# A build-time list scheduler for a two-layer hybrid trunk: a shared-port rule for VectorE and GpSimd, and matmul prices from measurement

## The chip, the cores and the metric

The kernel runs on one core of a Trainium2 chip. The metric is the device time of one execution in microseconds (us), as a median over several runs. The engines are named as the profile names them: PE is TensorE's matmul stream and PEld its weight loads, DVE is VectorE, ACT is ScalarE, POOL is GpSimd, SP is SyncE, which issues all the DMAs here.

## The reference, cut to what matters

A float32 input of 1024 tokens by 1024 channels passes through two layers of the same form and a last RMSNorm. Cut to its outline:

```python
for l in range(2):
    h = rmsnorm(x, norm_mix[l])
    parts = split(h @ w_in[l])
    y_a = rglru_mixer(...)    # causal convolution, gated linear recurrence
    y_b = nsa_mixer(...)      # compressed, selected and sliding-window attention
    y_c = gla_mixer(...)      # gated linear attention in chunks
    y_d = mla_mixer(...)      # latent attention
    x = x + groupwise_rmsnorm(y_a, y_b, y_c, y_d) @ w_out[l]
    h = rmsnorm(x, norm_ffn[l])
    gate, up = split(h @ w_gate_up[l])
    x = x + (silu(gate) * up) @ w_down[l]
return rmsnorm(x, final_norm)
```

## The kernel before, in words

**Precision.** Most products are made of three passes over operands that are split in a high and a low part (fp32r): ACT casts the source to the high part, DVE subtracts that from the source and writes the low part (`split`, line 382). One such split of a 128x512 tile therefore costs one ACT and one DVE instruction. Some sources lie in PSUM (then the DVE subtraction has one SBUF operand), others in SBUF (then it has two).

**Stages of a layer.** (1) The input norm and the first projections; (2) gated linear attention (`z_stream`, `gla_levels`, `gla_out`, from line 776), whose products are in plain float32, with projections of other mixers as filler for PE; (3) compression of keys and values, and projections; (4) latent attention (`mla_a`, `mla_t`, `mla_pv`); (5) sparse attention (`nsa_a`, `nsa_t`, `nsa_pv`); (6) the rest of the output projection beside the second norm (`h_stream`, `forms`, from line 1905), which writes the seven Strassen-like forms of the normed input; (7) the gate and up projections, as seven half-size products per 256 columns (`mat`, line 2149), whose weight forms are made by `prepare` (line 2059): GpSimd adds or subtracts two weight blocks in SBUF (a 128x512 product, tiles `utmp`, `qtmp` and `stg`), then ACT and DVE split the result; (8) the down projection in the same manner (`chunks`, line 2286), where both operands must be split. The last columns follow (`down`), and after the second layer the final norm (`finish`, line 2394).

**What sets the order.** Nothing is reordered on the chip: each engine runs its own list of instructions in order. These lists are written at build time by the class `Flow` (line 175), a list scheduler with a clock per engine. DVE, ACT and POOL operations are put in with a priority, a price and their dependences (`do`, line 193; `D_` and `P_` in lines 297 to 301 set the prices, 0.07 us + n/960 on DVE for n columns). PE work comes from generators ("streams") that yield the time at which they can go on, and book the price of what they issued with `f.pe(price)` (line 199). `run` (line 226) takes again and again the candidate with the smallest key, and emits it:

```python
c = self.clk.get(eng, 0.0)
r = when(o[3], eng)
key = (max(c, r + load), o[0], r, o[1])
```

that is the earliest start by the planner's clock, then the priority (a small number first), then the time at which its inputs were ready, then the order of entry. `when` (line 78) adds a latency to what another engine made: 0.12 us on the same engine, 0.26 us towards PE, 0.19 us otherwise. So a price has no effect on the chip but through the order in which instructions of one engine stand, and through the choice of buffers and PSUM banks, which goes by the same clock. The arithmetic of all RMSNorms goes through `rstd_of` (line 441): DVE writes `ms`, GpSimd raises it to the power -0.5 (`rstd`), and a DVE operation scales the rows by it.

Of the kernel before, what the change touches and what calls it, by code (L numbers as in the profile page):

```python
# [76 lines left out]

def when(x, eng):
# [7 lines left out]
    return 0.0 if x is None or x is True else float(x)  # L86

# [87 lines left out]
class Flow:  # L175
# [7 lines left out]

    def __init__(self):
        self.clk = {}
        self.t = 0.0
        self.streams = []
        self.ops = {}
        self.n = 0
        self.tag, self.prio = None, 0  # L190
        self.table = ("Exp", "Tanh")

    def do(self, eng, cost, deps, func, a, k, table=None):
        self.n += 1
        ev = Ev(eng)
        self.ops.setdefault(eng, []).append((self.prio, self.n, cost, deps, func, a, k, ev, self.tag, table))
        return ev
# [28 lines left out]
    def run(self, until):  # L226

        while not until():
            best = None
            for eng, q in self.ops.items():  # L230
                c = self.clk.get(eng, 0.0)
                for o in q:
                    r = when(o[3], eng)
                    load = 1.28 if o[9] is not None and o[9] != self.table else 0.0
# [15 lines left out]
            else:  # L250
# [5 lines left out]
                self.clk[eng] = o[7].t = start + o[2]  # L256
                o[4](*o[5], **o[6])  # L257

@with_exitstack
def kernel(ctx: ExitStack, tc: tile.TileContext, I: dict, out: bass.AP, dbg=None):  # L260
# [180 lines left out]
    def rstd_of(ss, n, count, deps):  # L441
# [3 lines left out]
        return r, P_(172, e, G.tensor_tensor, r[:, :n], ms[:, :n], negh[:, :n], ALU.pow)  # L445
# [134 lines left out]
    def cm(g, m, evac, last=False):  # L580
# [3 lines left out]
        for k in range(NK):  # L584
# [8 lines left out]
            te = f.pe(6 * 0.216)  # L593
# [41 lines left out]
    def start_stage(l, ready, load, gain, hp, bufs, bd, vpl, tables=0.0, done=None):  # L635
# [36 lines left out]
        def g2(gq):  # L672

            for hf in range(2):
                cs = slice(hf * 512, (hf + 1) * 512)
                for m in range(2):
# [3 lines left out]
                    for k in range(NK):  # L680
# [6 lines left out]
                        te = f.pe(3 * 0.216)  # L687
# [53 lines left out]
    for l in range(DEPTH):  # L741
# [34 lines left out]
        def z_stream():  # L776
# [4 lines left out]
            for hf in range(2):  # L781
# [11 lines left out]
                tg = D_(512, f.pe(0.858), V.tensor_scalar, z[:, cs], pz, par["bg2"], -320.0, ALU.add, ALU.max)  # L793
# [5 lines left out]
            for hf in range(2):  # L799
# [32 lines left out]
        def a_stream(c, xc, tx):  # L832
            tg, tt = [], []
            for gi in range(2):
                tg.append(ap.tile([P, SEQ], F32, tag=f"tg{gi}", name=f"tg{gi}"))
                for hf in range(2):
# [4 lines left out]
                    e = A_(512, [f.pe(0.858), par["done"]], S.activation, tg[gi][:, cs], pg, AF.Tanh, bias=halfb[:, c, gi:gi + 1],  # L841
# [11 lines left out]
            e = D_(1024, e, V.tensor_tensor_scan, xc, a, ti, 0.0, ALU.mult, ALU.add)  # L853
# [85 lines left out]
        def gla_levels():  # L939
# [3 lines left out]
            for t in range(NT):  # L943
                for li in range(5):
# [34 lines left out]
        def gla_out():  # L979
# [3 lines left out]
            for t in range(NT):  # L983
# [6 lines left out]
                if t < NT - 1:  # L990
# [13 lines left out]
                    td = D_(256, f.pe(0.432), V.tensor_tensor, ds, dsv,  # L1004
# [11 lines left out]
                te = f.pe(1.29)  # L1016
# [126 lines left out]
        def compress():  # L1143
# [5 lines left out]
            for j in range(2):  # L1149
# [11 lines left out]
                for u in range(4):  # L1161
# [4 lines left out]
                    for q_ in range(4):  # L1166
# [8 lines left out]
                        te = f.pe(0.22)  # L1175
# [36 lines left out]
            te = f.pe(0.7)  # L1212
# [1273 lines left out]
```

## Time and profile before

| | us |
|---|---|
| median of 3 runs | 2569.16 |
| lowest and highest of them | 2566.72, 2569.29 |
| the profiled execution, its own time | 2567.09 |
| its span, first to last instruction | 2565.0 |
| PE busy in the span | 2486.2 |
| DVE busy | 1907.0 |
| ACT busy | 1234.1 |
| POOL busy | 716.3 |

The profiled execution lies 2.07 us under the median. Busy time on PE is the union of matmuls whose ends are modelled, so a PE that counts as busy may still be waiting for short times between two matmuls. The mean granted clock of PE over the span was 0.990.

### The profile page before, as it was taken

Reading aid. Unit: us, or ns where it says so; the run is one execution under the profiler, and the core shown is the slowest. Engines: PE = TensorE matmul, PEld = TensorE weight load, DVE = VectorE, ACT = ScalarE, POOL = GpSimd, SP = SyncE. Lnnn points to the kernel's source line nnn. Section 1 sums busy time; section 2 is a strip of 40 time slices with the busy share of each in tenths; the row PEclk is TensorE's granted clock in tenths of the full one; section 3 lists DMA queues with packets and bytes.
Section 4 is the critical chain, followed back from the end, with each engine's and each line's share of the span. In section 5 each row is a group of like instructions: output and inputs, shape, how many; then the busy total and the mean of one; then the engine's idle time right before and its main releaser. Section 6 shows DMA issues by size and latency. Waiting matters only on the chain.

```text
span 2565.0 us, 35737 instructions
## 1 busy us (share of the span) xinstructions
PE 2486.2 (97%) x12629; PEld 2077.9 (81%) x12629; DVE 1907.0 (74%) x3654; ACT 1234.1 (48%) x2727; POOL 716.3 (28%) x698
## 2 busy tenths in 40 slices
PE   8999899998999999999999998999989999999998
PEld 7777788887888888778887787888878888887786
DVE  7985987787665665798769768877776566667976
ACT  5444587874333333444344446877653333334443
POOL 2010111223333333543110101212143333336422
PEclk9999999999999999999999999999999999999999
DMA  4011102221232333543310111031302332335432
GB/s 156 17 46 43 53 26 81 65 85 36 87 107 95 107 104 97 211 162 99 123 65 17 62 35 46 26 95 54 116 22 82 115 115 79 111 121 196 156 91 91
DMA packets 137410, 224.05 MB, mean 87 GB/s; under 512 B 13552, under 2 KB 83600, under 8 KB 134672
## 3 DMA queue, kind: packets, MB, share of 16 engines
q1 hardware_dynamic: 137232, 221.77, 26.3%
q8 instruction: 100, 1.64, 0.3%
q14 instruction: 78, 0.64, 0.1%
HBM read 164.07 MB, written 49.28 MB: 83 GB/s over the span
## 4 chain that ended last, share of the span: by engine, by line
PE 83%; DVE 9%; ACT 3%; issue 2%; DMA 1%; SPq 1%; POOL 1%; DVEq 0%; POOLq 0%; ACTq 0%
PE ps L2167 32%; PE ps L2308 13%; PE ps L609 7%; PE ps L1796 4%; PE ps L1345 4%; PE ps L590 3%; PE ps L1739 2%; PE ps L1720 2%; DVE T L257 2%; PE ps L685 2%; PE ps L628 2%; PE ps L2333 1%; PE ps L1536 1%; PE ps L1512 1%; DVE x_res L257 1%
## 5 line engine op out<-in xcount | busy, mean ns | idle before, releaser
L2167 PE MATMUL ps<-T,wu 128*128 128x512 f32 (+1 forms) x2160 | 498.6, 386 | 3.1 <-ACT qtmp L257 1.8
L2167 PEld LDWEIGHTS ps<-T,wu 128*128 128x128 f32 x2160 | 401.2, 189 | 86.6 <-ACT qtmp L257 2.0
L2167 PE MATMUL ps<-h,wu 128*128 128x512 f32 (+1 forms) x1656 | 386.0, 386 | 0.5 <-DVE wu L257 0.5
L2167 PEld LDWEIGHTS ps<-h,wu 128*128 128x128 f32 x1656 | 302.2, 188 | 68.9 <-DVE wu L257 0.7
L257 POOL TENSOR_TENSOR rstd<-ms,negh 128x1 f32<-128x1 f32 (+1 forms) x152 | 100.0, 661 | 778.8 <-DVE ms L257 778.4
L2308 PE MATMUL ps<-T 128*128 128x512 f32 x1176 | 275.7, 390 | 3.9 <-DVE x_res L257 3.8
L2308 PEld LDWEIGHTS ps<-T 128*128 128x128 f32 x1176 | 220.8, 188 | 52.9 <-DVE x_res L257 4.2
L609 PE MATMUL ps<-w,T 128*128 128x512 f32 (+1 forms) x1152 | 250.9, 366 | 2.1 <-DVE KS L257 1.1
L257 ACT CAST wu<-stg 128x512 fp32r<-128x512 f32 x220 | 136.2, 619 | 189.3 <-PE ps L2167 80.3
L609 PEld LDWEIGHTS ps<-w,T 128*128 128x128 f32 x1152 | 191.5, 189 | 35.4 <-issue 4.3
L257 POOL TENSOR_TENSOR utmp<-stg,stg 128x512 f32<-128x512 f32 x84 | 114.5, 1364 | 344.6 <-DVE wu L257 130.5
L257 DVE TENSOR_TENSOR wu<-stg,wu 128x512 fp32r<-128x512 f32 x214 | 182.4, 852 | 14.2 <-ACT wu L257 14.2
L1796 PE MATMUL ps<-w,T 128*128 128x512 f32 x768 | 190.7, 396 | 0.0
L257 DVE TENSOR_TENSOR wu<-utmp,wu 128x512 fp32r<-128x512 f32 x134 | 110.2, 823 | 107.9 <-ACT wu L257 101.3
L257 DVE TENSOR_TENSOR x_res<-x_res,ps 128x512 f32<-128x512 f32 x224 | 143.2, 678 | 34.9 <-PE ps L2308 18.5
L1796 PEld LDWEIGHTS ps<-w,T 128*128 128x128 f32 x768 | 140.4, 188 | 26.9
L257 DVE TENSOR_TENSOR pts<-ps,pts 128x512 fp32r<-128x512 f32 x212 | 140.8, 685 | 26.9 <-ACT pts L257 25.5
L257 ACT CAST wu<-utmp 128x512 fp32r<-128x512 f32 x134 | 83.2, 621 | 118.2 <-POOL utmp L257 118.2
L257 POOL TENSOR_TENSOR stg<-stg 128x512 f32<-128x512 f32 x88 | 129.9, 1495 | 3.5
L257 ACT CAST pts<-ps 128x512 fp32r<-128x512 f32 x212 | 118.2, 591 | 16.3 <-PE ps L1720 12.9
L257 ACT CAST T<-stg 128x512 fp32r<-128x512 f32 x116 | 70.9, 621 | 105.8 <-PE ps L2308 91.3
L257 DVE TENSOR_TENSOR T<-stg,T 128x512 fp32r<-128x512 f32 x108 | 102.7, 957 | 25.3 <-ACT T L257 25.0
(378 smaller groups left out, 4799.5 us busy)
## 6 DMA issues: line engine op xcount, KB each, us to landing
stg<-in_w_gate_up_dram SPq DMA_DIRECT2D x88, 512.0 KB, 3.9
stg<-af SPq DMA_DIRECT2D x70, 512.0 KB, 3.6
af<-so SPq DMA_DIRECT2D x20, 1024.0 KB, 6.1
stg<-in_w_in_dram SPq DMA_DIRECT2D x36, 512.0 KB, 3.5
br<-in_w_down_dram SPq DMA_DIRECT2D x24, 512.0 KB, 6.5
af<-sg SPq DMA_DIRECT2D x20, 512.0 KB, 2.7
stg<-in_cmp_w_dram SPq DMA_DIRECT2D x16, 512.0 KB, 3.9
stg<-in_w_out_dram SPq DMA_DIRECT2D x16, 512.0 KB, 3.9
```

The lines of the kernel that those rows point to most:

```text
L257: o[4](*o[5], **o[6])
L590: PE.matmul(o[:, hf * 512:(hf + 1) * 512], lhsT=w[:, a], rhs=T[:, b, k, hf * 512:(hf + 1) * 512], start=(k == 0 and i == 0), stop=(k == NK ...
L609: PE.matmul(o[j][:, :g.n], lhsT=T[:, a, k, t * P:(t + 1) * P], rhs=g.of(k)[:, b, :], start=(k == 0 and i == 0), stop=(k == NK - 1 and i == 2))
L628: PE.matmul(o[:, :g.n], lhsT=T[:, a, k, t * P:(t + 1) * P], rhs=g.of(k)[:, b, :], start=(k == 0 and i == 0), stop=(k == NK - 1 and i == 2))
L685: PE.matmul(o, lhsT=w[:, a], rhs=T[:, b, k, cs], start=(k == 0 and i == 0), stop=(k == NK - 1 and i == 2))
L1345: PE.matmul(st[:, o0:o0 + wp_], lhsT=lh, rhs=rh[:, k0 + c0:k0 + c0 + wp_], start=(i == 0), stop=(i == len(ops) - 1), skip_group_check=True)
L1512: PE.transpose(pt[:, (2 * j + i) * P:(2 * j + i + 1) * P], Pm[:, i, kb * P:(kb + 1) * P], ident)
L1720: PE.transpose(pt[:, h * P:(h + 1) * P], Ps[h // 2][:, h % 2, kb * P:(kb + 1) * P], ident)
L1739: PE.matmul(ot, lhsT=VS[:, kb0 + kb, br].rearrange("p a d -> p (a d)"), rhs=R["npts", t, br, kb][:, a], start=(kb == 0 and a == 0), stop=( ...
L1796: PE.matmul(o, lhsT=T[:, a, 2 * u + k, t * P:(t + 1) * P], rhs=w.w[:, b_, k * 512:k * 512 + 512], start=(n == 0), stop=(n == 6 * len(us) - 1))
L2167: PE.matmul(bk[b, i][:, cs], lhsT=u[:, x, k * P:(k + 1) * P], rhs=H[n][:, y, k, cs], skip_group_check=True, start=(start and k == 0 and s ...
L2308: PE.matmul(o, lhsT=a[:, x, t * P:(t + 1) * P], rhs=b[:, y], skip_group_check=True, start=(new and s == 0), stop=(k == k0 + nk - 1 and s = ...
```

## The change

The planner alone is changed; each engine gets the same instructions. (1) The scheduler has a `port` with an end time for DVE and one for POOL. A DVE operation that reads two SBUF operands (or a `tensor_scalar` or `tensor_copy` from SBUF to SBUF of 64 columns or more) may not start before the last GpSimd `tensor_tensor` ends, and the other way round; the power of `rstd_of` is such a `tensor_tensor`. (2) Prices of PE are set to `mm(n)` and `mm4(n)`: a 512-column pass from 0.216 to 0.2267 us, a plain float32 product of 512 columns from 0.858 to 0.4297 us, of 256 columns from 0.432 to 0.2163 us. (3) The price of a DVE scan is doubled, and the power on four columns goes from 0.51 to 0.99 us. The latencies of `when` are kept. `LAG` and `MORE` are defined and not used, and the class `Ev` is defined a second time with the same body.

```diff
+LAG = {"DVE": 0.12, "ACT": 0.14, "POOL": 0.08, "PE": 0.19}
+MORE = {"PE": 0.03, "POOL": 0.06}
+def mm(n):
+    return (n + 32) / 2400
+def mm4(n):
+    return max(n / 1200 + 0.003, 0.112)
...
+        self.port = {"DVE": 0.0, "POOL": 0.0}
...
-    def do(self, eng, cost, deps, func, a, k, table=None):
+    def do(self, eng, cost, deps, func, a, k, table=None, port=False):
...
                     r = when(o[3], eng)
+                    if o[10]:
+                        r = max(r, self.port["POOL" if eng == "DVE" else "DVE"])
...
                 self.clk[eng] = o[7].t = start + o[2]
+                if o[10]:
+                    self.port[eng] = start + o[2]
...
+    def sbuf(x):
+        return isinstance(x, bass.AP) and getattr(x, "space", None) != PSUM
     def D_(n, deps, func, *a, **k):
-        return f.do("DVE", 0.07 + n / 960, deps, func, a, k)
+        name = getattr(func, "__name__", "")
+        two = (name in ("tensor_tensor", "tensor_tensor_scan") and sbuf(a[1]) and sbuf(a[2])
+               or name == "scalar_tensor_tensor" and sbuf(a[1]) and sbuf(a[3])
+               or name in ("tensor_scalar", "tensor_copy") and sbuf(a[0]) and sbuf(a[1]) and n >= 64)
+        return f.do("DVE", 0.07 + n / 960, deps, func, a, k, None, two)
     def P_(n, deps, func, *a, **k):
-        return f.do("POOL", 0.15 + n * 0.0021 if n <= 512 else 0.28 + n * 0.00154, deps, func, a, k)
+        return f.do("POOL", 0.15 + n * 0.0021 if n <= 512 else 0.28 + n * 0.00154, deps, func, a, k, None,
+                    getattr(func, "__name__", "") == "tensor_tensor")
...
-        return r, P_(172, e, G.tensor_tensor, r[:, :n], ms[:, :n], negh[:, :n], ALU.pow)
+        return r, P_(172 if n == 1 else 400, e, G.tensor_tensor, r[:, :n], ms[:, :n], negh[:, :n], ALU.pow)
...
-            te = f.pe(6 * 0.216)
+            te = f.pe(6 * mm(512))
...
-                    tz.append(D_(128, t1, V.tensor_tensor_scan, b[:, ct], ones, e[:, ct], 0.0, ALU.mult, ALU.add))
+                    tz.append(D_(256, t1, V.tensor_tensor_scan, b[:, ct], ones, e[:, ct], 0.0, ALU.mult, ALU.add))
...
-            e = D_(1024, e, V.tensor_tensor_scan, xc, a, ti, 0.0, ALU.mult, ALU.add)
+            e = D_(2048, e, V.tensor_tensor_scan, xc, a, ti, 0.0, ALU.mult, ALU.add)
...
-                        te = f.pe(0.858)
+                        te = f.pe(mm4(512))
...
-                        te = f.pe(0.432)
+                        te = f.pe(mm4(256))
...
-                te = f.pe(1.29)
+                te = f.pe(4 * mm4(64) + mm4(256))
...
-                        te = f.pe(0.44)
+                        te = f.pe(4 * mm(256))
...
-                te[n, i] = f.pe(12 * 0.0025 + 12 * (cs.stop - cs.start) / 2400)
+                te[n, i] = f.pe(12 * mm(cs.stop - cs.start))
...
-                            te = f.pe(3 * 0.2165)
+                            te = f.pe(3 * mm(512))
```

The other `f.pe` prices are changed in the same manner.

## Rows read from the trace of the kernel before

**Rows 1.** The page, part 1 (busy, share, instructions) and part 4 (the chain).

```profile
PE 2486.2 (97%) x12629; PEld 2077.9 (81%) x12629; DVE 1907.0 (74%) x3654; ACT 1234.1 (48%) x2727; POOL 716.3 (28%) x698
PE 83%; DVE 9%; ACT 3%; issue 2%; DMA 1%; SPq 1%; POOL 1%; DVEq 0%; POOLq 0%; ACTq 0%
```

**Rows 2.** Windows of layer one: us, PE, PEld, DVE, ACT, POOL busy, clock, DMA.

```profile
60.00:174.00 114.00, 113.18 (x507) 88.82 (x506) 100.64 (x338) 48.34 (x160) 11.68 (x14) 1.00 0.10 31
258.00:316.00 58.00, 51.39 (x389) 47.40 (x390) 54.55 (x126) 35.26 (x78) 6.21 (x14) 0.99 0.17 52
430.00:589.00 159.00, 157.47 (x955) 136.79 (x954) 120.58 (x277) 115.03 (x264) 36.22 (x45) 1.00 0.30 93
589.00:651.00 62.00, 53.02 (x261) 43.56 (x261) 52.70 (x89) 33.90 (x63) 26.39 (x23) 0.92 0.03 9
651.00:1066.00 415.00, 415.00 (x1844) 340.85 (x1845) 259.20 (x341) 138.15 (x242) 152.74 (x110) 1.00 0.33 111
1066.00:1154.00 88.00, 81.69 (x345) 65.97 (x344) 82.01 (x99) 40.63 (x71) 50.07 (x33) 0.96 0.52 178
```

**Rows 3.** Waits of PE, whole span: us in total, times, longest.

```profile
PE ps L1943 <- DVE ms L257: 11.9, 2, 6.0
PE ps L2308 <- DVE wu L257: 7.9, 2, 3.9
```

**Rows 4.** Chain pieces (start, us, what), and one PE group in 60 to 174 us.

```profile
171.12 3.49 PE ps L840 x8
...
1154.32 113.23 PE ps L2308 x498
...
L609 PE MATMUL ps<-w,T 128*128 128x512 f32 x192 | 53.3, 419 | 0.0
```

**Rows 5.** DVE groups by shape, whole span: busy us, mean ns of one.

```profile
L257 DVE TENSOR_TENSOR T<-ps,T 128x512 fp32r<-128x512 f32 x64 | 42.5, 684 | 12.9 <-ACT hn L257 11.2 <-ACT T L257 1.5
L257 DVE TENSOR_TENSOR T<-utmp,T 128x512 fp32r<-128x512 f32 x48 | 53.1, 1107 | 0.9 <-ACT T L257 0.9
```

**Rows 6.** POOL groups by shape, whole span.

```profile
L257 POOL TENSOR_TENSOR utmp<-stg,stg 128x512 f32<-128x512 f32 x84 | 114.5, 1364 | 344.6 <-DVE wu L257 130.5 <-DMA stg<-in_w_gate_up_dram 121.5 <-issue 63.9
L257 POOL TENSOR_TENSOR rstd<-ms,negh 128x1 f32<-128x1 f32 x136 | 83.7, 618 | 622.2 <-DVE ms L257 621.8
L257 POOL TENSOR_TENSOR rstd<-ms,negh 128x4 f32<-128x4 f32 x16 | 16.4, 1026 | 156.7 <-DVE ms L257 156.7
```

**Rows 7.** Timeline of the second norm, around 630 us (start, us, engine, operation).

```profile
627.32 1.64 POOL L257 TENSOR_TENSOR utmp<-stg 128x512 f32<-128x512 f32 x1 [1.23 <-DVE wu L257]
627.77 1.75 DVE L257 TENSOR_TENSOR h<-hn,h 128x512 fp32r<-128x512 f32 x1
629.43 0.68 DVE L257 TENSOR_TENSOR x_res<-x_res,ps 128x512 f32<-128x512 f32 x1
630.03 0.68 DVE L257 TENSOR_TENSOR h<-hn,h 128x512 fp32r<-128x512 f32 x1
630.63 0.68 DVE L257 TENSOR_TENSOR wu<-stg,wu 128x512 fp32r<-128x512 f32 x1
631.24 1.27 DVE L257 SCALAR_TENSOR_TENSOR hn<-x_res,rstd,ps 128x1024 f32<-128x1024 f32 x1
...
632.65 1.73 PE L1943 MATMUL ps<-ident,hn 128*128 128x128 f32 x7 [5.94 <-DVE ms L257]
```

**Rows 8.** Timeline at the start of the down projection, around 1085 us.

```profile
1083.54 4.02 DVE L257 TENSOR_TENSOR T<-stg,T 128x512 fp32r<-128x512 f32 x3
...
1087.49 0.68 DVE L257 TENSOR_TENSOR wu<-utmp,wu 128x512 fp32r<-128x512 f32 x1
```

**Rows 9.** Timeline of the end, from 2549 us.

```profile
2549.77 1.77 POOL L257 TENSOR_TENSOR x_res<-x_res,gfin 128x512 f32<-128x512 f32 x1 [0.99 <-ACT x_res L257]
...
2550.31 1.25 DVE L257 SCALAR_TENSOR_TENSOR ms<-ss 128x1 f32<-128x1 f32 x1
```

**Rows 10.** Timeline around 612 us: a power on POOL beside DVE.

```profile
612.27 0.94 POOL L257 TENSOR_TENSOR rstd<-ms,negh 128x1 f32<-128x1 f32 x1 [1.29 <-DVE ms L257]
612.71 0.68 DVE L257 TENSOR_TENSOR T<-stg,T 128x512 fp32r<-128x512 f32 x1
```

More of the change, by code (lines that the diff above doesn't have):

```diff
@@ L75, in __init__ @@
         self.eng, self.t = eng, t
+class Ev:
+    __slots__ = ("t", "eng")
+    def __init__(self, eng, t=INF):
+        self.eng, self.t = eng, t
+LAG = {"DVE": 0.12, "ACT": 0.14, "POOL": 0.08, "PE": 0.19}
+MORE = {"PE": 0.03, "POOL": 0.06}
 def when(x, eng):
@@ L190, in __init__ @@
         self.tag, self.prio = None, 0
+        self.port = {"DVE": 0.0, "POOL": 0.0}
         self.table = ("Exp", "Tanh")
-    def do(self, eng, cost, deps, func, a, k, table=None):
+    def do(self, eng, cost, deps, func, a, k, table=None, port=False):
         self.n += 1
         ev = Ev(eng)
-        self.ops.setdefault(eng, []).append((self.prio, self.n, cost, deps, func, a, k, ev, self.tag, table))
+        self.ops.setdefault(eng, []).append((self.prio, self.n, cost, deps, func, a, k, ev, self.tag, table, port))
         return ev
@@ L791, in z_stream @@
                 PE.matmul(pz, lhsT=wg2, rhs=glrT[:, cs], start=True, stop=True)
-                tg = D_(512, f.pe(0.858), V.tensor_scalar, z[:, cs], pz, par["bg2"], -320.0, ALU.add, ALU.max)
+                tg = D_(512, f.pe(mm4(512)), V.tensor_scalar, z[:, cs], pz, par["bg2"], -320.0, ALU.add, ALU.max)
                 banks.give(pz, tg)
@@ L840, in a_stream @@
                     PE.matmul(pg, lhsT=wbd[:, gi, c], rhs=xc[:, cs], start=True, stop=True)
-                    e = A_(512, [f.pe(0.858), par["done"]], S.activation, tg[gi][:, cs], pg, AF.Tanh, bias=halfb[:, c, gi:gi + 1],
+                    e = A_(512, [f.pe(mm4(512)), par["done"]], S.activation, tg[gi][:, cs], pg, AF.Tanh, bias=halfb[:, c, gi:gi + 1],
                            scale=0.5)
@@ L1003, in gla_out @@
                     ds = lt.tile([P, 4, 64], F32, tag="ds", name="ds")
-                    td = D_(256, f.pe(0.432), V.tensor_tensor, ds, dsv,
+                    td = D_(256, f.pe(mm4(256)), V.tensor_tensor, ds, dsv,
                               bdmask.unsqueeze(2).to_broadcast([P, 4, 64]), ALU.mult)
@@ L1174, in compress @@
                                   start=False, stop=(lp == 15), skip_group_check=True)
-                        te = f.pe(0.22)
+                        te = f.pe(2 * mm(256))
                     w.done(te)
@@ L1211, in compress @@
                           start=(hh == 0), stop=(hh == 1))
-            te = f.pe(0.7)
+            te = f.pe(4 * mm4(64))
             R["KC"] = key_stack(64, te, KC, pk[:, 0:64], NSA_SCALE)
@@ L1299, in kv_stream @@
                     PE.matmul(pk, lhsT=wukv[:, a, h * P:(h + 1) * P], rhs=ct[:, b_], start=(i == 0), stop=(i == 2))
-                ek = key_stack(512, f.pe(0.648), KN[:, h, cs], pk, MLA_SCALE)
+                ek = key_stack(512, f.pe(3 * mm(512)), KN[:, h, cs], pk, MLA_SCALE)
                 R["kn", hf].append(ek)
@@ L1308, in kv_stream @@
                               rhs=wukv[:, b_, 512:768], start=(i == 0), stop=(i == 2), skip_group_check=True)
-            te = f.pe(1.3)
+            te = f.pe(12 * mm(256))
             pv4 = pv.rearrange("p (t h d) -> p t h d", t=4, h=4)
@@ L1346, in scores @@
                               start=(i == 0), stop=(i == len(ops) - 1), skip_group_check=True)
-                    te = f.pe(wp_ / 2400 + 0.003)
+                    te = f.pe(mm(wp_))
             return te
@@ L1645, in nsa_c @@
                               start=False, stop=(a == 1), skip_group_check=True)
-            te = f.pe(0.95)
+            te = f.pe(8 * mm4(64) + mm(256))
             sv = st[:, :256].rearrange("p (h c) -> p h c", h=4)
@@ L1741, in nsa_pv @@
                                   start=(kb == 0 and a == 0), stop=(kb == nkb - 1 and a == 1))
-                    te = f.pe(0.43)
+                    te = f.pe(2 * mm(512))
                     ptl.give(te)
@@ L1798, in w_part @@
                         n += 1
-                    te = f.pe(0.648)
+                    te = f.pe(3 * mm(512))
                 if last:
@@ L2309, in chunks @@
                                           start=(new and s == 0), stop=(k == k0 + nk - 1 and s == 2))
-                            te = f.pe(3 * 0.2165)
+                            te = f.pe(3 * mm(512))
                             if k == k0 + nk - 1:
@@ L2334, in down @@
                                       start=(j == 0 and i == 0), stop=(j == 1 and i == 2))
-                    te = f.pe(6 * 0.2165)
+                    te = f.pe(6 * mm(512))
                     cs = slice(hf * 512, (hf + 1) * 512)
```

1 line of the change is left out of this document (removed).

## The prediction

> **What bounds the kernel now.** I read the page first. PE is busy for 2486.2 of 2565.0 us and makes 83% of the chain that ended last [rows 1]. So the whole stake is PE's idle time, 2565.0 - 2486.2 = 78.8 us, and the short gaps that the busy count hides. Second, the windows by stage [rows 2]: the reader is to see that the idle time is not spread evenly. The gate and up stage (651 to 1066 us) has PE busy for 415.00 of 415 us: no order can gain there. The second norm (589 to 651) leaves 62 - 53.02 = 9.0 us idle, the compression (258 to 316) 58 - 51.39 = 6.6, the start of the down projection (1066 to 1154) 88 - 81.69 = 6.3, sparse attention (430 to 589) 1.5, gated linear attention (60 to 174) 0.8. The idle stages are those in which DVE is nearly full: 54.55 of 58, 82.01 of 88, 100.64 of 114 us. Third, the waits of PE [rows 3]: the longest end on DVE, in the second norm (11.9 us in two waits, one per layer) and on a split at the start of the down projection (7.9 us in two). So the change matters where the order of DVE's list decides when PE goes on.
>
> **What the new prices say, against the trace.** 498 passes of the down projection ran in 113.23 us, 227.4 ns each; eight plain float32 products of 512 columns in 3.49 us, 436 ns each [rows 4]. The planner books 216 and 858 ns for them, after the change 226.7 and 429.7. Both new prices are right to 2%; the old ones were 5% too low and twice too high.
>
> The port rule has its ground too. A 512-column subtraction with its source in PSUM takes 684 ns; the same with its source in SBUF, made by POOL, 1107 ns on average [rows 5], and one that ran into a POOL product took 1.75 us [rows 7]. The product itself takes 1364 ns [rows 6]. The chip does keep the two apart, and the old planner, which books 0.60 us for every split, does not know it. But the exclusion is there with or without the rule: the rule saves nothing by itself. What it can do is to put a DVE operation that reads PSUM into the time of a POOL product, instead of a blocked split with work queued behind it.
>
> **The change part by part.** The instructions are the same on each engine and SP's transfers too; only places in the lists, buffers and PSUM banks move. So each term is a wait that gets shorter or longer.
>
> Gated linear attention. Per tile of 128 tokens the planner books 4 x 0.432 + 0.858 + 1.29 = 3.88 us for products that it will book at 4 x 0.2163 + 0.4297 + 0.664 = 1.96 us; over eight tiles 15.4 us of PE time per layer that the chip never needed. With it gone, the planner sees that PE runs dry earlier and puts filler passes there. What is to gain: the 192 filler passes of that window took 53.3 us, 278 ns each [rows 4], against 227 in a steady run, so 192 x 0.0502 = 9.6 us are hidden waits, and 0.8 us is idle: 10.4 us per layer is the end on the side of gain. The end on the side of loss is one more DVE split of 0.68 us in front of each tile's chain, 8 x 0.68 = 5.4 us. DVE is 88% busy in that window [rows 2], so most of these gaps wait for DVE itself, which no order of PE fills: I take a fifth of the gain, -2.0 per layer.
>
> Second norm. PE stood 5.94 us before the transposes at 632.65 [rows 7]. In front of the scaling (`hn`) that releases them, DVE's list has a split that the `utmp` product blocked (1.75 instead of 0.68 us), the residual add out of PSUM, a split, and a weight split. With the port rule the add can be planned into the time of the product, so that it (0.60 us from start to start) no longer stands behind the blocked split, and the weight split of lower priority (0.61 us) moves behind the scaling: -1.2 per layer. POOL will still start its product when its inputs are there, so the blocked 1.07 us stay. Ends: -(1.07 + 0.60 + 0.61) = -2.3, and +1.75 if one more blocked split comes in front.
>
> Start of the down projection. Three splits in a row took 4.02 us, instead of 3 x 0.68 = 2.04, and the split for which PE waited came behind them [rows 8]. The planner still picks by readiness and not by need; I take half of the excess, -1.0 per layer. Ends: -3.9, the whole wait [rows 3], and +1.3, one more such split. The later part of that stage is out of reach: its 498 passes run without a gap [rows 4].
>
> End of the kernel. A DVE operation on one column took 1.25 us because a POOL product of 1.77 us ran, with the residual add behind it [rows 9]. Two SBUF operands mark it for the rule: -0.6, between -1.25 and 0.
>
> At nothing: the gate and up stage, covered by PE's 415 of 415 us; if that cover went, a weight unit late by one blocked split would cost 1.75 us each time. The 5% on all passes in the attention stages, where PE's clock and the others' move together: -1.5 (all idle time of the sparse-attention window) to +7 per layer (ten operations of 0.684 us in front of an evacuation). The compression: its waits are chains in DVE's nearly full time; from -6.6 to one split, +0.7. The doubled price of the scans and the longer power (1026 ns measured on four columns, 0.99 booked from now on [rows 6]) touch 8 + 2 and 8 operations per layer: nothing, as their consumers follow behind other DVE work.
>
> Sum: 2 x (-2.0 - 1.2 - 1.0) - 0.6 = **-9.0 us**. The profiled execution took 2567.09 us, so 2558.1 by its own time; it lies 2.07 us under the median of the runs, from which the change is measured, so 2569.16 - 9.0 = 2560.2, forecast as **2560**.
>
> **A rule weighed.** While a power ran on POOL (0.94 us instead of the usual 0.618), DVE's split of two SBUF operands took its plain 0.68 us [rows 6, 10]. So POOL paid, and DVE did not. The Trainium skill (SBUF — State Buffer, Who interferes with whom) says that a DVE instruction with two SBUF inputs contends with a GpSimd instruction that reads SBUF, and that whichever issues first holds the shared pair for the whole instruction while the other fully blocks. The blocked split of 1.75 us agrees with it, the split beside the power does not; by the page the planner is right to keep splits off the powers, the second rival below loses its ground, and the sum stays -9.0; by the row the ban is a planning error at each of 152 places.
>
> **The rivals.** First, no measurable change: the order is set by data, not by prices. For it: the norm's waits are chains (add, sum of squares, power, scaling, transposes), and half the span is without a gap. Against it: the double price in gated linear attention must move filler. It gives 2564 to 2574. That the change doesn't do what it says belongs here: if the test of operands missed most operations, only PE's prices would act.
>
> Second, slower by the rule itself. The key takes the earliest start, then the priority, then the readiness, and an engine's readiness contains the other's port but not its own: on a tie, whichever engine has just held the port keeps it as long as it has older work. So in the plan powers and products wait behind a backlog of splits, and what follows from them (the scaling, the next unit's split) is written behind that backlog in DVE's list; on the chip POOL is done early and its result waits. There are 136 + 16 powers [rows 6]. For it: splits beside a power are not slowed on the chip [rows 10], so the plan delays powers for nothing. Against it: DVE operations on PSUM leave windows. Place: the second norm, once PE has no filler, which is where it stood 5.94 us already. Price: one blocked split (1.75 us) in front of the scaling for four of the eight tiles, 7.0 us per layer, 14.0 in all, with half of the sum above kept: 2569.16 + 14.0 - 4.5 = 2579. It decides from the point at which the norm's idle time passes 9.0 us by more than the other terms give back.
>
> Third, slower by half a correction: passes are booked 5% longer, the latencies are not shortened, so PE's results come later in the plan than on the chip and other DVE and ACT work is written in front of the evacuations. Ten exposed places per layer at 0.684 us [rows 5] are 13.7 us: 2569.16 + 13.7 - 4.5 = 2578. Against it: PE idles for only 1.5 of 159 us in sparse attention, so there is slack.
>
> Fourth, much faster: filler falls into all hidden gaps of gated linear attention and the other terms reach their ends, 2 x (-10.4 - 2.3 - 3.9) - 1.25 = -34.5: 2535.
>
> **How the numbers follow.** About 0.2% (5.1 us) is what a measurement of this kernel can tell from no change. Chances: forecast 0.36 (its own range 2545 to 2564, half the gain of the first stage and all of the others at the lower end), much faster 0.13, no measurable change 0.17, slower by the rule 0.20, slower by half a correction 0.14. So faster 0.49, same 0.17, slower 0.34. The range that holds 8 in 10 reaches from the forecast to both sides: 2542 to 2582.
>
> **What would show it.** Right: the 192 filler passes near 60 to 174 us cost under 270 ns each; PE's wait before the transposes of the second norm falls under 5 us per layer; its wait on a split at the start of the down projection under 3.9. DVE's residual adds start during `utmp` products. Wrong: more idle time of PE in the norm, scalings behind several splits after a finished power (second rival); more and longer waits of PE in the attention stages (third); gaps in the 415 us stage.

## The result: 1.3% slower, and the profile after

The changed kernel took 2600.96 us (median of 4 runs, 2598.85 to 2605.83), against 2569.22 for the kernel before: a ratio of 1.0128 (95% interval 1.0116 to 1.0140), +32 us. The forecast was 2560 with a range to 2582, so its sign was wrong. The profiled execution is the longest of the four (2605.83 us), so the differences by stage below add up to 39 us and not to 32.

The page of the changed kernel, part 1 (busy), as in [rows 1]:

```profile
PE 2503.5 (96%) x12629; PEld 2092.1 (80%) x12629; DVE 1898.7 (73%) x3654; ACT 1235.8 (47%) x2727; POOL 729.4 (28%) x698
```

The instructions are as many as before. PE idles 2604.1 - 2503.5 = 100.6 us (78.8 before), and it is busy 17.3 us longer with the same work. Where, the windows tell. The columns are those of [rows 2], of the changed kernel; the later stages start 13 to 22 us later than before:

```profile
60.00:174.00 114.00, 107.39 (x459) 84.05 (x458) 92.70 (x314) 43.99 (x147) 7.34 (x9) 0.96 0.09 28
160.00:180.00 20.00, 15.90 (x41) 10.66 (x42) 15.33 (x45) 3.65 (x15) 2.58 (x3) 0.66 0.00 1
180.00:200.00 20.00, 20.00 (x92) 15.83 (x92) 11.93 (x20) 10.96 (x18) 3.30 (x4) 1.00 0.00 0
325.00:435.00 110.00, 99.04 (x656) 88.35 (x655) 89.81 (x227) 82.05 (x217) 16.12 (x41) 0.95 0.07 20
435.00:610.00 175.00, 171.79 (x1027) 148.45 (x1026) 128.15 (x313) 120.97 (x290) 38.07 (x46) 0.99 0.32 96
610.00:673.00 63.00, 54.41 (x274) 45.57 (x274) 48.72 (x80) 34.88 (x65) 26.32 (x23) 0.95 0.03 9
673.00:1088.00 415.00, 414.69 (x1839) 339.98 (x1838) 265.07 (x351) 139.10 (x242) 155.03 (x110) 1.00 0.32 111
```

In gated linear attention PE now idles 114 - 107.39 = 6.6 us (0.8 before) and issues 459 instead of 507 matmul records in the same time. DVE is *less* busy there, 92.70 against 100.64 us. Between 160 and 180 us PE issues 41 records and the granted clock is 0.66 on average, so for most of that time it is at the lower of its two levels (1.2 instead of 2.4 GHz). The kernel before had 89 records at full clock in that slice:

```profile
160.00:180.00 20.00, 20.00 (x89) 15.01 (x89) 14.43 (x34) 11.20 (x21) 5.96 (x9) 1.00 0.06 14
```

The slice from close by, PE's timeline of the changed kernel. L627 and L646 are filler (L590 and L609 before), the others are products of gated linear attention:

```profile
152.06 1.02 PE L997 MATMUL ps<-Qz,kt 128*128 128x256 f32 x4
...
153.16 3.10 PE L627 MATMUL ps<-T,w 128*128 128x512 f32 x12
156.10 1.02 PE L994 MATMUL ps<-Qb,kt 128*128 128x512 f32 x2
157.39 1.00 PE L1051 MATMUL ps<-vc,at 128*128 128x64 f32 x8
...
161.68 4.26 PE L997 MATMUL ps<-Qz,kt 128*128 128x256 f32 x8 [3.29 <-DVE at L286]
...
173.79 0.31 PE L1033 MATMUL ps<-ident,kd 128*128 128x128 f32 x1 [2.07 <-DVE kd L286]
174.04 2.31 PE L627 MATMUL ps<-T,w 128*128 128x512 f32 x6
...
176.64 2.49 PE L627 MATMUL ps<-T,w 128*128 128x512 f32 x6
...
183.65 5.74 PE L627 MATMUL ps<-T,w 128*128 128x512 f32 x24
```

The next piece of L627, from the chain:

```profile
190.65 24.70 PE ps L627 x108
```

After 156 us there is no filler until 174. It is not used up: of the 192 passes of L627 in layer one (four tiles of 48), one tile is out by 156 us, and the other 144 come from 174 us on (6 + 6 + 24 + 108). In the kernel before the second tile starts at 163.72 us, at once behind the first. PE waits 3.29 us for DVE, and the eight records after the wait (four products: a plain float32 product leaves two records, as shown further below) take 4.26 us, 0.53 each, against 1.02 us for four records at 152 us, 0.26 each. Until then it was DVE that had waited. DVE's longest wait in the stage, of the changed kernel:

```profile
DVE at L286 <- PE ps L1051: 7.4, 4, 2.4
```

It was 0.8 us in two waits before. So filler is issued ahead of the products for which DVE waits, and its next tile comes too late to cover PE's own waits. PE's waits that answer to [rows 3], of the changed kernel (L1980 was L1943, L2345 was L2308):

```profile
PE ps L1980 <- DVE ms L286: 11.4, 2, 5.7
PE ps L2345 <- DVE T L286: 11.1, 4, 4.3
```

The stalls that the forecast wanted to shorten are all but unchanged. For the accounting I cut each trace at the last product of a stage and took the difference to the kernel before, both layers together (one profiled execution each, so single entries under 2 us mean little; that of "all but the float32 prices" lies 6 us under its median):

| kernel | gated linear att. and projections | compression, latent keys | latent att. | sparse att. | second norm | gate/up | down | sum, with the end |
|---|---|---|---|---|---|---|---|---|
| the change | +18.6 | +1.7 | +8.2 | +11.0 | -1.8 | +1.2 | +0.8 | +39.1 |
| port rule alone | +1.0 | -5.1 | +6.2 | +6.5 | -2.4 | -1.1 | +3.1 | +8.3 |
| all prices, no port rule | +20.5 | +1.2 | +16.6 | +5.7 | +7.5 | +60.0 | -5.3 | +104.8 |
| all but the float32 prices | +4.7 | -7.8 | +10.0 | +5.3 | -1.8 | +1.0 | -1.4 | +9.6 |
| float32 prices alone | +21.2 | -1.5 | +0.6 | +5.3 | -0.4 | +1.5 | +0.5 | +27.2 |
| gate/up price alone | +0.7 | +1.0 | +0.6 | 0.0 | +0.2 | +60.7 | +0.1 | +64.4 |
| attention prices alone | -0.5 | +0.8 | +18.6 | +5.2 | -0.3 | 0.0 | -0.6 | +23.0 |
| change, filler at 0.25 us | +1.9 | +5.2 | +7.3 | +9.1 | -1.8 | +1.1 | 0.0 | +22.3 |
| DVE +0.1 ns | +6.7 | +1.5 | +2.7 | 0.0 | +0.3 | 0.0 | -0.3 | +10.8 |

### The profile page after: what moved, and what is told of

Read it like the earlier page. It is cut to its first block, busy times and chain, and to the rows that moved or that the text cites. A ratio compares the mean times of both kernels' runs of the same rounds, so it can differ in the third digit from the quotient of the medians.

```text
span 2604.1 us, 35648 instructions
## 1 busy us (share of the span) xinstructions
PE 2503.5 (96%) x12629; PEld 2092.1 (80%) x12629; DVE 1898.7 (73%) x3654; ACT 1235.8 (47%) x2727; POOL 729.4 (28%) x698
## 4 chain that ended last, share of the span: by engine, by line
PE 83%; DVE 9%; ACT 4%; issue 2%; DMA 1%; SPq 1%; POOL 0%; DVEq 0%; POOLq 0%; ACTq 0%
PE ps L2204 31%; PE ps L2345 14%; PE ps L646 8%; PE ps L1833 6%; PE ps L627 3%; PE ps L1382 3%; PE ps L1776 2%; PE ps L1757 2%; PE ps L722 2%; DVE T L286 2%; PE ps L2370 1%; PE ps L665 1%; PE ps L997 1%; ACT Pm L286 1%; PE ps L1573 1%
## 5 line engine op out<-in xcount | busy, mean ns | idle before, releaser
L2345 PE MATMUL ps<-T 128*128 128x512 f32 x1176 | 276.4, 392 | 3.9 <-DVE T L286 2.6
L2345 PEld LDWEIGHTS ps<-T 128*128 128x128 f32 x1176 | 221.5, 189 | 52.9 <-DVE T L286 3.2
L646 PE MATMUL ps<-w,T 128*128 128x512 f32 (+1 forms) x1152 | 251.2, 367 | 1.3 <-ACT tg L286 1.3
L286 DVE TENSOR_TENSOR wu<-stg,wu 128x512 fp32r<-128x512 f32 x214 | 208.4, 974 | 44.5 <-ACT wu L286 44.0
L646 PEld LDWEIGHTS ps<-w,T 128*128 128x128 f32 x1152 | 192.5, 190 | 33.1 <-issue 1.7
L286 POOL TENSOR_TENSOR utmp<-stg 128x512 f32<-128x512 f32 x48 | 65.8, 1370 | 169.8 <-DMA stg<-in_w_gate_up_dram 68.3
```

What stands on the lines that cost most here:

```text
L646: PE.matmul(o[j][:, :g.n], lhsT=T[:, a, k, t * P:(t + 1) * P], rhs=g.of(k)[:, b, :], start=(k == 0 and i == 0), stop=(k == NK - 1 and i == 2))
L2345: PE.matmul(o, lhsT=a[:, x, t * P:(t + 1) * P], rhs=b[:, y], skip_group_check=True, start=(new and s == 0), stop=(k == k0 + nk - 1 and s = ...
```

## The experiments

Four theories. **A**: the float32 products of gated linear attention, booked at half of the price before, let the planner issue too much filler there. **B**: the port rule is at fault. **C**: passes booked 5% longer with the latencies kept write other work in front of what PE waits for. **D**: any disturbance of the prices costs some us. All ratios are to runs of the kernel before on the same chip.

**Half the change at a time.** First the port rule alone (prices as before):

> The port rule alone, with all the old prices. Theory A (the halved prices of the plain float32 products make the planner put too much filler into gated linear attention) expects little here: between -5 and +8 us against the kernel before. Theory B (the port rule itself delays powers and splits in the plan) expects most of the +32 here: +20 or more. Theory C (passes booked 5% longer with the latencies kept) expects 0. Theory D (any disturbance of the prices scatters the result, nothing adds up) expects anything between -10 and +15.

2575.27 us, ratio 1.0027 (1.0016 to 1.0037). Second, all the prices without the rule:

> All new prices (passes, plain float32 products, scans, power), without the port rule. Theory A: +15 to +30, with PE dry at the end of gated linear attention. Theory B: 0 to +8. Theory C: +15 to +30, with PE's added waits in latent and sparse attention. Theory D: between -10 and +15.

2672.38 us, ratio 1.0413 (1.0384 to 1.0441): none of the theories had this. Third, everything except these two edits and their like:

```diff
-                        te = f.pe(0.858)
+                        te = f.pe(mm4(512))
...
-                        te = f.pe(0.432)
+                        te = f.pe(mm4(256))
```

> The whole change, but the plain float32 products keep their old prices (0.858 and 0.432 us). Theory A: the +12 and +6 us of the two gated linear attention stages go away, so +10 to +18 instead of +32. Theory B and theory C: still +25 or more. Theory D: anything, not to be told from e4 by a sum.

2583.01 us, ratio 1.0055 (1.0040 to 1.0070). Fourth, these edits alone:

> The prices of the plain float32 products alone are new, all else is as before. Theory A: +12 to +25, with the window of gated linear attention longer by 6 to 12 us per layer and PE idle after its filler has run out. Theories B and C: within 3 us of the kernel before. Theory D: between -10 and +15.

2592.68 us, ratio 1.0098 (1.0083 to 1.0113). Its stage of gated linear attention is longer by 12.4 us in layer one and 8.8 in layer two, and it has the same dry slice:

```profile
160.00:180.00 20.00, 14.52 (x45) 10.65 (x46) 14.15 (x40) 3.96 (x16) 3.21 (x4) 0.66 0.00 1
```

(These edits also take one price of sparse attention from 0.95 to 1.016 us and one of compression from 0.7 to 0.448.) So A holds for most of the loss, and B falls: the rule alone costs 7 us, and without it the prices cost 104. But 7 + 104 is not 32: the parts don't add. Which of the two float32 prices the chip takes is worked out in the section on the prediction: the old one.

**What the rule hides: 60 us.** Of the prices, that of the gate and up products alone, no rule:

```diff
-                te[n, i] = f.pe(12 * 0.0025 + 12 * (cs.stop - cs.start) / 2400)
+                te[n, i] = f.pe(12 * mm(cs.stop - cs.start))
```

> Of the whole change only the price of the gate and up products is new (12 passes of 512 columns booked at 2.72 instead of 2.59 us); no port rule. Theory C, in the sharper form that the prices-only kernel suggests (PE's results come later in the plan than on the chip, so weight splits are written in front of the DVE addition that PE waits for): +50 to +85 us, nearly all between the first and the last of the gate and up products, with PE waiting for the addition in PSUM. Theory A and theory B: within 3 us, as this line was costed at nothing. Theory D: between -10 and +15.

2631.91 us, ratio 1.0248 (1.0231 to 1.0266): +63 us from the one line, nearly all of it in its stage. Its group of products on the page has 46.8 us of idle time before it (the rest of the 60.7 us was not followed up):

```profile
L2191 PE MATMUL ps<-h,wu 128*128 128x512 f32 (+1 forms) x1656 | 400.5, 394 | 46.8 <-DVE ps L281 44.9
```

One of the ten such waits in layer one, on the timeline of that kernel:

```profile
819.21 1.29 POOL L281 TENSOR_TENSOR utmp<-stg 128x512 f32<-128x512 f32 x1 [9.91 <-DMA stg<-in_w_gate_up_dram]
...
820.53 0.62 ACT L281 CAST wu<-utmp 128x512 fp32r<-128x512 f32 x1 [4.54 <-POOL utmp L281]
821.06 0.61 ACT L281 CAST wu<-stg 128x512 fp32r<-128x512 f32 x1
...
821.58 1.07 ACT L281 ACTIVATE sg<-ps 128x512 f32<-128x512 f32 x2
...
822.40 0.69 DVE L281 TENSOR_TENSOR ps<-ps,qtmp 128x512 f32<-128x512 f32 x1
...
823.14 3.07 PE L2191 MATMUL ps<-h,wu 128*128 128x512 f32 x12 [2.27 <-DVE ps L281]
```

The same place in the kernel before, where PE does not wait:

```profile
809.88 0.60 ACT L257 ACTIVATE sg<-ps 128x512 f32<-128x512 f32 x1 [1.33 <-PE ps L2167]
...
810.51 0.70 DVE L257 TENSOR_TENSOR ps<-ps,qtmp 128x512 f32<-128x512 f32 x1 [1.99 <-ACT sg L257]
810.62 1.30 POOL L257 TENSOR_TENSOR utmp<-stg 128x512 f32<-128x512 f32 x1 [9.68 <-DMA stg<-in_w_gate_up_dram]
...
811.96 0.62 ACT L257 CAST wu<-utmp 128x512 fp32r<-128x512 f32 x1 [0.97 <-POOL utmp L257]
```

In both, POOL's product waits some 10 us for its weights. Before, ACT's evacuation `sg` stands ahead of the cast of that product, follows PE at once, and the addition in PSUM that PE needs next is early. With the longer price two casts stand in front of `sg`; ACT idles 4.54 us for the product, and `sg`, the addition and PE follow behind. By the planner's key this fits a plan in which PE's result comes later, so that the cast goes first; the plan itself is not on record. With the port rule the stage takes what it took before (+1.2 us in the change, +1.0 without the float32 prices), and in the changed kernel `sg` stands ahead of that cast again (831.77 and 833.50 us). How the rule brings this about was not looked at. So the order that C names does occur, in a stage that had been costed at nothing, and the whole change escapes it by its other half.

**The other half of the correction.** The whole change, with the latencies that it defines and does not use:

```diff
-        return x.t + (0.12 if x.eng == eng else 0.26 if eng == "PE" else 0.19)
+        return x.t + LAG.get(x.eng, 0.19) + (0.0 if x.eng == eng else MORE.get(eng, 0.0))
```

> The whole change with the latencies that it defines and does not use (0.12, 0.14, 0.08, 0.19 us by the engine that made the value, 0.03 more towards PE, 0.06 towards GpSimd). If the half correction is the cause of what is left beside gated linear attention (theory C), the stages after it win back their 8 to 14 us: 2575 to 2592, and more if the shorter latencies also keep filler from gated linear attention. Theory A: the +18 us of gated linear attention stay, so not under 2585. Theory D: anything between 2560 and 2620.

2607.66 us, ratio 1.0152 (1.0137 to 1.0167). Sparse attention comes back (+1.2 instead of +11.0), latent attention gets worse (+18.0 instead of +8.2), gated linear attention too (+25.5). Kept latencies are not the cause as a whole.

**How the filler can be held back.** Two forms of A, on the whole change. First, filler passes at 0.25 us, which lies 10% above the 0.227 of a steady run:

```diff
-            te = f.pe(6 * mm(512))
+            te = f.pe(6 * 0.25)
...
-                te[j] = f.pe(3 * (0.0025 + g.n / 2400))
+                te[j] = f.pe(3 * (0.0365 + g.n / 2400))
```

> The whole change, and the filler passes of the projections booked at 0.25 us, as bundles of 18 of them ran beside gated linear attention (4.48 us). If the double price of the float32 products had been making up for a filler price that was too low (theory A, form 1: two errors that cancelled), the planner puts about 14% fewer passes between two products, the filler lasts longer, and 8 to 15 of the +18 us come back: 2586 to 2594. If the filler ends early for another reason (form 2: its next tile waits for a pair of PSUM banks), less than 5 us come back: 2596 to 2604.

2592.96 us, ratio 1.0092 (1.0077 to 1.0107). In its profiled execution gated linear attention is at +1.9 us instead of +18.6, and the dry slice is gone:

```profile
160.00:180.00 20.00, 19.98 (x92) 14.76 (x91) 13.58 (x32) 10.77 (x21) 4.27 (x6) 1.00 0.06 14
```

(By medians 8 us came back, not 17: the profiled execution of the change was its slowest, this one is near its fastest.) Second form, the DVE operations that free a filler tile's two PSUM banks get priority 0:

```diff
         def ax_evac(c, px, te):
+            old, f.prio = f.prio, 0
...
             banks.give(px, e)
+            f.prio = old
```

> The whole change, and the operations that free the pair of PSUM banks of a filler tile (one on ACT, then three additions of 1.27 us on DVE for the convolution, or the four of the gate) get the highest priority instead of the lowest. Theory A, form 2: the dry stretch of PE near 158 to 178 us shrinks by 6 to 12 us in layer one and as much as that in layer two: 2582 to 2593. Form 1: the additions only move in front of the gated linear attention's own chain, which then ends later: 2598 to 2606.

2595.28 us, ratio 1.0105 (1.0090 to 1.0120), the stage at +10.7, and the dry slice is shorter:

```profile
160.00:180.00 20.00, 16.93 (x64) 12.05 (x65) 15.73 (x39) 11.15 (x21) 1.69 (x2) 0.91 0.00 1
```

That the next filler tile waits for its banks is a part of the dry slice. In the profiled executions the filler's price does more (+1.9 against +10.7); the medians, 2.3 us apart with intervals that overlap, do not tell the two apart. The pair of prices (float32 halved, filler at 0.25) by itself, on the kernel before:

> The kernel before, with the new prices of the plain float32 products and filler passes at 0.25 us, nothing else. If two errors had cancelled, and both are now right, gated linear attention takes what it took before, and the whole 2568 to 2578. If the new float32 price is bad by itself: 2585 or more, as with it alone.

2576.95 us, ratio 1.0028 (1.0016 to 1.0041), the stage at +1.0. (Some 5 us of what its profiled execution loses lie in sparse attention.) The time came out as expected, but not for the reason given: the halved float32 price loses 21 us in its stage alone and 1.0 beside a filler price that is too high. Two errors do make up for each other here, but they are errors of this kernel. The kernel before had the float32 price right and the filler price 5% too low.

**Price changes that say nothing.** The kernel before, with 0.07 made 0.0701 in DVE's price:

> The kernel before, with every DVE price raised by a tenth of a nanosecond: a change that says nothing about the chip. Theory D (the planner is so sensitive that any change of a price moves the result by several us, and the order of the kernel before happens to be a good one): +2 to +12 us. Theories A and C (only prices that are off by much matter): within 2 us of the kernel before.

2576.79 us, ratio 1.0024 (1.0014 to 1.0034). And 1 ns more on each ACT operation:

> The kernel before, with every ACT price raised by one nanosecond: a second change that says nothing. Theory D: +2 to +12 us, with other stages hit than by the tenth of a nanosecond on DVE. Theories A and C: within 2 us.

2573.32 us, ratio 1.0009 (1.0000 to 1.0019). They lose 7.0 and 7.5 us in the same place, gated linear attention of layer two, and not in different ones as theory D had it. There, PE's timeline of the kernel with the tenth of a nanosecond, and its window, with that of the kernel before behind it:

```profile
1419.52 1.00 PE L1014 MATMUL ps<-vc,at 128*128 128x64 f32 x8
1423.96 1.10 PE L960 MATMUL ps<-Qz,kt 128*128 128x256 f32 x4 [3.44 <-DVE at L257]
1425.95 2.10 PE L960 MATMUL ps<-Qz,kt 128*128 128x256 f32 x4 [0.89 <-DVE Qz L257]
```

```profile
1340.00:1445.00 105.00, 99.55 (x444) 78.19 (x443) 90.95 (x305) 43.90 (x154) 11.41 (x14) 0.97 0.10 31
```

```profile
1340.00:1445.00 105.00, 103.84 (x475) 82.68 (x474) 94.42 (x313) 44.04 (x156) 13.80 (x18) 1.00 0.10 33
```

It is the same dry slice in small: the kernel before seems to stand right at its edge. Theory D holds, at the size of 4 to 7 us.

**The attentions.** The new prices of three kinds of products there, alone (5% more for 512 columns, 9% for the `0.44`), and the same products 5% shorter than before:

```diff
-                    te = f.pe(wp_ / 2400 + 0.003)
+                    te = f.pe(mm(wp_))
...
-                        te = f.pe(0.44)
+                        te = f.pe(4 * mm(256))
...
-                    te = f.pe(0.43)
+                    te = f.pe(2 * mm(512))
```

> The kernel before, with the new prices for the products of latent and sparse attention alone (the scores, and both products with the values). Theory C (passes booked longer with the latencies kept push other work in front of evacuations): +6 to +14 us, in the windows of the two attentions. Theory D: +0 to +12, and not more there than the price changes that say nothing. If 5% has no effect in these stages: within 2 us.

2589.06 us, ratio 1.0071 (1.0056 to 1.0086): +19.4 us, more than any theory had, most of it in latent attention (+18.6).

> The kernel before, with the same products of latent and sparse attention booked 5% shorter than before. If the loss has a direction (a price that is long writes other work in front of what PE waits for): -4 to +4 us, the two attentions no longer than before. If any displacement costs (theory D, in its strong form): +10 to +20 us.

2581.01 us, ratio 1.0045 (1.0030 to 1.0060), with +6.7 us in latent and +5.6 in sparse attention. So both sides lose, and C's direction is not shown here. What happens with the longer price: the chain of waits through latent attention of layer one, by line, first of that kernel, then of the kernel before:

```profile
by line: PE ps L1369 15.1%; PE ps L1560 8.9%; issue 7.7%; PE ps L1536 7.0%; ACT Pm L281 7.0%; DVE Pm L281 6.2%; PE ps L1447 5.9%; DVE pts L281 4.5%; ACT pts L281 4.2%; DVE qxy L281 4.2%; DVE mq L281 4.0%; ACT mq L281 3.6%; ACT qq L281 2.0%;
```

```profile
by line: PE ps L1345 24.2%; PE ps L1536 14.2%; PE ps L1512 12.5%; PE ps L1423 8.6%; ACT Pm L257 3.2%; DVE pts L257 3.1%; PE ps L1466 2.7%; ACT mq L257 2.7%; DVE Pm L257 2.6%; PE ps L1556 2.3%; PE ps L1465 2.2%; issue 2.0%; PE ps L456 1.6%;
```

Scores (L1345, now L1369), products with the values (L1536, now L1560) and transposes (L1512, now L1536) made 51% of the chain and make 31%. The softmax's `Pm` on ACT and DVE went from 6 to 13%. That PE has lost the work that covered it is a reading of the chain; no run isolates it.

**The powers.** The whole change, with the powers left out of the rule:

```diff
-                    getattr(func, "__name__", "") == "tensor_tensor")
+                    getattr(func, "__name__", "") == "tensor_tensor" and a[-1] != ALU.pow)
```

> The whole change, but the 152 powers of GpSimd are left out of the port rule. Theory B (the rule keeps splits off powers that do not slow them, so scalings are written behind a backlog): 8 to 15 us less than the whole change, 2586 to 2593, with the second norm shorter. If the powers do not matter: 2597 to 2605. Theory D: anything between 2590 and 2612.

2598.76 us, ratio 1.0110 (1.0094 to 1.0125): the interval overlaps that of the whole change. In the second norm it is at -2.6 and -2.8 us, the whole change at -1.0 and -0.8.

**Do the terms add up?** The whole change, old prices for the three attention products, filler at 0.25 us:

> The whole change, with the old prices for the products of the two attentions, and filler passes at 0.25 us. If the terms add up, what is left is the part that price changes without meaning cost as well: 2573 to 2582. If the stages act on each other in another way: 2585 or more.

2584.29 us, ratio 1.0060 (1.0045 to 1.0075). Of +32, 16 are left, between the two expectations. Sparse attention keeps +6.7 and gated linear attention +4.7. What in the rest causes the former was not isolated: the port rule alone costs +6.5 there and the float32 prices alone +5.3, this kernel has both, and they do not add.

**Direction.** The gate and up products booked shorter, by 5%, 10% and 2.5%, on the kernel before:

> The kernel before, with the gate and up products booked 5% shorter. If the loss has a direction: the stage stays at 430 and 428 us from its first to its last product, and the whole within 3 us, but for what theory D costs elsewhere (+4 to +7). If any displacement costs: +20 us or more in this stage.

> The kernel before, with the gate and up products booked 10% shorter. Direction: -6 to +2 us, the stage of these products at 426 to 431 us, the start of the down projection no longer than before. Any displacement costs, or the -4 was chance: +4 to +15.

> The kernel before, with the gate and up products booked 2.5% shorter. Direction: -5 to +2 us. Any displacement costs, or the -4 was chance: +4 to +15.

2564.73 us, ratio 0.9983 (0.9974 to 0.9992); 2572.19, 1.0014 (1.0006 to 1.0023); 2567.27, 0.9997 (0.9988 to 1.0006). The stage itself stays within 0.4 us of its time in all of them, so of the four prices tried without the port rule only the longer one hurts it. The first is the one kernel faster than both. It gains at the start of the down projection, PE's wait of that kernel that was 7.9 us in [rows 3]:

```profile
PE ps L2308 <- DVE wu L257: 3.3, 2, 1.7
```

But it is not a trend: 10% shorter has that wait at 7.5 us and loses. So the gain is put down to an order that fell well by chance; no run tests that.

## Why the prediction was wrong

**Gated linear attention** (forecast -2.0 per layer, measured +13.1 and +5.5). This is the step that failed, in its sign, and it failed in the reading of a price. The prediction took the `x8` of `L840` in [rows 4] for eight products of 436 ns and called both new prices "right to 2%". They are eight records of four products. The program calls that product 16 times (two layers, two tiles, two gates, two halves), and that of L957 16 times (two layers, eight tiles); the trace of the kernel before has twice as many records. A filler pass has one: L590 is called 48 times in each of eight tiles.

```profile
L840 PE MATMUL ps<-xc,wbd 128*128 128x512 f32 x32 | 14.5, 596 | 0.0
L957 PE MATMUL ps<-Qb,kt 128*128 128x512 f32 x32 | 16.6, 599 | 0.1
L590 PE MATMUL ps<-T,w 128*128 128x512 f32 x384 | 91.7, 396 | 0.1
```

So a plain float32 product of 512 columns takes two records of 0.43 us, 0.86 in all, and one of 256 columns 0.43: the old prices, 0.858 and 0.432, were right, and the new ones are half of what the chip takes. The "15.4 us of PE time per layer that the chip never needed" were needed. "With it gone, the planner sees that PE runs dry earlier and puts filler passes there" came true, but on the chip PE was still busy with the products. What the runs showed in place of the gain: the halved prices alone cost 24 us, and the whole change with the old ones back costs 14.6 instead of 32. The products for which DVE waits come late (7.4 us instead of 0.8), the first tile of L627 is out 7 us sooner than before, and between 156 and 174 us PE stands without filler, in part at the lower clock. The prediction had bounded the loss by DVE splits (5.4 us).

The 278 ns per filler pass [rows 4] were read as hidden waits to be won. They are not waits either. Rows of the kernel before, not used then:

```profile
122.69 1.72 PE L609 MATMUL ps<-w,T 128*128 128x512 f32 x6
124.25 0.59 PE L960 MATMUL ps<-Qz,kt 128*128 128x256 f32 x2
124.49 1.04 PE L609 MATMUL ps<-w,T 128*128 128x512 f32 x3
125.37 0.59 PE L960 MATMUL ps<-Qz,kt 128*128 128x256 f32 x2
125.62 2.44 PE L609 MATMUL ps<-w,T 128*128 128x512 f32 x9
127.89 1.02 PE L957 MATMUL ps<-Qb,kt 128*128 128x512 f32 x2
128.35 1.27 PE L609 MATMUL ps<-w,T 128*128 128x512 f32 x3
129.46 0.27 PE L996 MATMUL ps<-ident,kd 128*128 128x128 f32 x1
```

From the start of a bundle to the next product, behind a product of 256 columns: 3 passes 0.88 us, 6 passes 1.56, 9 passes 2.27. Behind one of 512 columns, 3 passes take 1.11. Beyond 0.227 a pass that is about 0.2 and 0.43 us, one record of the product ahead, and the product looks shorter by as much (0.24 us from 124.25 to 124.49). A round of six passes and one product, 122.69 to 124.49, is 1.80 us, and 6 x 0.227 + 0.43 = 1.79. So a pass costs there what it costs in a steady run. At these prices the records of the window of 60 to 174 us add up to about 111 of its 113.2 busy us (an estimate from their counts): 2 us per layer are hidden, not 9.6. The sign named for this term, under 270 ns a pass, did not come either: 282 in the changed kernel.

**Attention stages** (costed at nothing, ends -1.5 to +7 per layer; measured +8.6 and +10.6 for both attentions together). Their place and size are close to the third rival, which had 13.7 in all (measured 19.2) and a chance of 0.14. Its reason holds only in part: prices 5% shorter lose too, and shorter latencies help one attention and hurt the other. "PE idles for only 1.5 of 159 us in sparse attention, so there is slack" was the wrong reading: little idle time on PE says that the order is good, not that it is robust.

**Gate and up** (nothing; measured +0.5 and +0.7). Right for the whole change, and for the wrong reason: 415 of 415 us busy was taken as a cover against any order, while one price in it costs 60.7 us when the port rule is absent.

**Second norm** (-1.2 per layer; measured -1.0 and -0.8). Right in size. But not by the sign named, a wait under 5 us before the transposes: that is 5.7. The second rival's backlog is there in small: without the powers in the rule the norm gains 1.6 and 2.0 us more. The Trainium skill (SBUF — State Buffer, Who interferes with whom) says that of two instructions which contend for the shared port the later one fully blocks; the split beside a power in [rows 10] had not, and the other three splits of 512 columns that start during a power in the kernel before took 0.68 to 0.69 us too. The run without the powers sides with the row in the norm, but the whole kernel does not tell the two apart.

**Start of the down projection** (-1.0 per layer; measured +0.1 and +0.7). Wrong: PE's waits there only changed their name, from `wu` 7.9 us to `T` 11.1 in all. **End** (-0.6; measured -0.5): right. **Nothing for the scans, powers and compression**: right for compression (with the latent keys +1.1 and +0.6); no run has the prices of scans and powers alone.

**The rule saves nothing by itself**: right, and to be seen in the run with the rule alone. Its DVE busy time and the mean of the splits that POOL's products had blocked (1107 ns in [rows 5]):

```profile
PE 2489.0 (97%) x12629; PEld 2082.4 (81%) x12629; DVE 1873.6 (73%) x3654; ACT 1238.4 (48%) x2729; POOL 718.7 (28%) x698
```

```profile
L286 DVE TENSOR_TENSOR T<-utmp,T 128x512 fp32r<-128x512 f32 x44 | 40.4, 918 | 1.8 <-ACT T L286 1.0
```

DVE is busy 33.4 us less than before (1907.0), so collisions did get fewer, and the kernel is 7 us slower.

## What to carry to other kernels

In a list scheduler a price is a statement about order. Before a price is read out of a trace, count the calls in the program against the records in the trace: here 16 calls left 32 records, and a right price was halved. A second price that is off can hide such an error, as the filler at 0.25 us did. Measure first what a price change without meaning does (here 4 to 7 us from 0.1 and 1 ns): a forecast of a smaller gain than that says nothing, and most of the disturbances tried here, in either direction, made this order slower. When a half of a change is tried alone, its stages may lose what the other half was hiding (here 60 us).

## What was not expected of the hardware

A plain float32 product leaves two matmul records, each of 0.43 us at 512 columns and 0.216 at 256; a pass over split operands leaves one, of 0.227 at 512. Where the two kinds alternate, the last record of the product counts to the bundle of passes behind it, so a bundle looks 0.2 or 0.43 us longer than its passes, and the whole round costs no more than its parts (the rows above). And a dry slice costs twice: PE's waits of 3.29 and 2.07 us come with float32 records (two to a product) at 0.53 instead of 0.26 us, with a mean granted clock of 0.66 over 20 us; in the next 20 us, with filler again, it is 1.00.
